# One-hot gate products written to neighbouring PSUM words, copied to SBUF by ScalarE and multiplied from there by VectorE

## The chip, the cores and the metric

The kernel runs on one core of a Trainium2 chip. The metric is the device time of one execution in microseconds (us). A core has the engines TensorE (PE, with its weight loads shown apart as PEld), VectorE (DVE), ScalarE (ACT), GpSimd (POOL) and SyncE (SP, which here only issues DMAs). Each engine works through a queue of instructions of its own.

## The reference, cut to what matters

The program is two transformer blocks on 256 tokens of width 1024. Only the end of the second block is touched by the change: a product-key expert layer with 16384 experts of which each token uses 8 x 16.

```python
s = einsum("thpd,hpnd->thpn", q, sub_keys)            # 8 heads, two halves of 128 keys
s_top, i_top = top_k(s, 16)
best, ci = top_k(s_top[..., 0, :, None] + s_top[..., 1, None, :], 16)
e = i1 * 128 + i2                                      # expert of token t, head h, rank k
gate = softmax(best)
act = gelu(einsum("thkd,td->thk", u_exp[e], xb))
out = einsum("thk,thkd->td", gate * act, v_exp[e])
```

## The kernel before, in words

The kernel gathers no expert. It computes gelu(u . x) for all 16384 experts and all 256 tokens, multiplies each by the gate that the token gives to that expert (zero for nearly all), and multiplies the result by all of v. The products of gelu are the *stash*: `ST[0]` and `ST[1]`, each 128 partitions x 64 experts x 256 tokens of float32, partition and column together being the expert's number.

The layer runs in three stages on TensorE:

- **u stage.** 64 chunks of 1 MB of `peer_u` come by DMA (`raw`). For each half chunk ScalarE rounds it to float32r (`whi`, line 128), VectorE computes the rest (`wlo`, line 129), and TensorE multiplies both parts with the tokens in 24 matmuls of 128x256 into the PSUM tile `mm`. ScalarE takes gelu of a chunk to the stash (line 1418 before, the same line after).
- **gates.** `weights8(half, t0)` makes the gates of 8 tokens for one half of the stash. There are 32 groups of 8 tokens and two halves, so 64 calls. VectorE builds one-hot matrices in the tile `one` (lines 1551, 1552) and multiplies one of them by the gate, which is split into three bfloat16 parts (line 1555, three times). TensorE multiplies them: for each token three accumulating bfloat16 matmuls with 128 weights columns (`B`) and 64 moving columns (`Aw`), 24 for a call and 1536 in all. Their result is the table of gates, 128 x 64 for each token, in one PSUM bank (tile `mb`, two of them). VectorE multiplies this bank with the stash in place (line 1562).
- **v stage.** The stash is split into two parts (`pTh` by ScalarE, `pTl` by VectorE, line 135), chunks of `peer_v` come and are split as those of u, and TensorE sums 12 matmuls of 128x512 for each half chunk into the tiles `acc`.

The gates of the first half are made while the second half of u is multiplied, those of the second half while the first half of v is. `one` has two buffers and `mb` two, so calls go in pairs: two calls are built, their 48 matmuls stand close together in TensorE's queue, and two multiplications follow. A pair's matmuls are mostly one run of 48 or 46 between the wide matmuls; the first one or two often stand alone.

The order within each engine's queue is set before the launch by a scheduler that works from a timeline of its own; `prio(...)` only shifts what it prefers. So an edit can move instructions that it does not name.

Of the kernel before, what the change touches and what calls it, by code (L numbers as in the profile page):

```python
# [10 lines left out]
F32 = mybir.dt.float32  # L11
# [4 lines left out]
AF = mybir.ActivationFunctionType  # L16
ALU = mybir.AluOpType
# [4 lines left out]
P = 128  # L22
# [39 lines left out]
def tile_kernel(ctx, tc, A, out, taps=None):  # L62
    nc = tc.nc
# [16 lines left out]
    def mmps(side=None):  # L80

        if side is None:
            turn[0] += 1
            side = turn[0] % turn[1] == 0
        if side:
            return psum.tile([P, 512], F32, name="mb", tag="mb", bufs=2)
        return psum.tile([P, 512], F32, name="mm", tag="mm", bufs=6)
# [4 lines left out]
    @contextmanager  # L92
    def prio(d):

        p = tc.cur_priority
        tc.cur_priority = max(0, p + d)
        try:
            yield
        finally:
            tc.cur_priority = p  # L100
# [44 lines left out]
    def mm(ps, lhsT, rhs, start, stop):  # L145
        nc.tensor.matmul(ps, lhsT, rhs, start=start, stop=stop, skip_group_check=True)  # L146
# [1250 lines left out]
    for c in range(3, 8):  # L1397
        hs = weights[c - 3] if c < 5 else q_halves(c)
        ps = mmps()
# [137 lines left out]
    def weights8(half, t0):  # L1537
        ps = mmps(True)
        n = 8
        one = pk.tile([P, n * 384], BF, name="one", tag="one", bufs=2)  # L1540
        B = one[:, :n * P].rearrange("p (t j) -> p t j", t=n)
        E = one[:, n * P:n * 192]
        Aw = one[:, n * 192:].rearrange("p (i t j) -> p i t j", i=3, t=n)

        def pairs(v, j):
            return v.rearrange("p (t j d) -> p t j d", t=n, d=2) if j is None else v.rearrange("p (j d) -> p j d", d=2)[:, None].to_broadcast([P, n, j, 2])

        def each(v, j):
            return v[:, t0:t0 + n, None, :].to_broadcast([P, n, j, 2])

        nc.vector.tensor_tensor(pairs(one[:, :n * P], None), pairs(iob, 64), each(iT[:, 1], 64), op=ALU.is_equal)
        nc.vector.tensor_tensor(pairs(E, None), pairs(iob[:, half * 64:(half + 1) * 64], 32), each(iT[:, 0], 32), op=ALU.is_equal)
        for i in range(3):
            o = n * 192 + i * n * 64
            nc.vector.tensor_tensor(pairs(one[:, o:o + n * 64], None), pairs(E, None), each(g3[:, i], 32), op=ALU.mult)
        po = ps.rearrange("p (i t) -> p i t", t=n)
        with prio(-2 * LOW):
            for t in range(n):
                for i in range(3):
                    mm(po[:, :, t], B[:, t, :], Aw[:, i, t, :], i == 0, i == 2)  # L1560
        v = ST[half][:, :, t0:t0 + n]
        nc.vector.tensor_tensor(v, po, v, op=ALU.mult)

    def v_split(c):
        half, o = c // 32, (2 * c) % 64
# [11 lines left out]
    with prio(LOW):  # L1577
        for t0 in range(0, T, 8):
            weights8(0, t0)
# [10 lines left out]
    with prio(LOW):  # L1590
        for t0 in range(0, T, 8):
            weights8(1, t0)
# [31 lines left out]
    for tt in range(NT):  # L1624
        ss = ev[:, 6 * D + 8 * tt:6 * D + 8 * tt + 2]
        for j in range(2):
            o = slice(j * 512, (j + 1) * 512)
            t = rt[tt][:, o]
# [102 lines left out]
```

## Time and profile before

| | |
|---|---|
| time, median of 3 runs | 1662.21 us (1661.76 to 1663.13) |
| profiled execution | 1662.13 us, span of the core 1660.4 us |
| granted TensorE clock | 0.999 of full speed |
| TensorE busy | 1637.8 us, 99% of the span |
| VectorE busy | 1183.4 us, 71% |
| ScalarE busy | 770.5 us, 46% |
| gate matmuls on TensorE | 1536, from 979 to 1434 us |

The span runs from the first to the last instruction; the 1.7 us between it and the profiled execution's time lie outside of it. TensorE's matmuls overlap and their ends are modelled, so the distance between the starts of matmuls tells more than their durations. A row of the timeline that ends in xN is N instructions of one kind with no idle time between them.

### The profile page before, as it was taken

The page shows a single profiled execution, that of the slowest core. Times are in us where ns is not written, and L with a number is a line of the kernel's source. Part 1 is how long each engine was busy: PE and PEld are TensorE (multiplying, and loading weights), DVE is VectorE, ACT ScalarE, POOL GpSimd, SP SyncE. Part 2 cuts the span into 40 slices and gives each one's busy share as a digit, 9 for nine tenths or more (in the row PEclk, how much of TensorE's full clock was granted, in tenths as well). Part 3 has the DMA queues.
Part 4 walks back from the last instruction along what each step waited for, and adds up shares of the span by engine and source line. Part 5 has one row for each costly group of instructions (what it writes and reads, how often), then busy time and mean ns, then how long its engine had stood idle before and what let it go on. Part 6 is the DMA issues. An engine that isn't in the chain of part 4 may idle for free.

```text
span 1660.4 us, 28789 instructions
## 1 busy us (share of the span) xinstructions
PE 1637.8 (99%) x12006; PEld 1515.3 (91%) x12006; DVE 1183.4 (71%) x1925; ACT 770.5 (46%) x1064; POOL 62.7 (4%) x114
## 2 busy tenths in 40 slices
PE   7999999999999999999999999999999999999997
PEld 7999999989999899998999999999999888888886
DVE  5768776666878676766799984877747888755555
ACT  5545444464544466653544444333344333454443
POOL 0000000200000010002000000000000000000001
PEclk9999999999999999999999999999999999999999
DMA  5739665235866455463535545344355434455553
GB/s 225 283 135 349 261 258 220 94 132 218 339 256 242 178 170 176 144 247 130 194 128 180 184 170 181 128 142 137 128 183 212 165 135 155 159 188 201 186 195 127
DMA packets 46274, 312.76 MB, mean 188 GB/s; under 512 B 6240, under 2 KB 6256, under 8 KB 10304
## 3 DMA queue, kind: packets, MB, share of 16 engines
q1 hardware_dynamic: 43344, 300.82, 50.7%
q0 software_dynamic: 2656, 9.06, 1.6%
q8 instruction: 94, 1.54, 0.4%
q10 hardware_dynamic: 144, 1.05, 0.2%
q14 instruction: 36, 0.29, 0.1%
HBM read 308.78 MB, written 2.12 MB: 187 GB/s over the span
## 4 chain that ended last, share of the span: by engine, by line
PE 95%; DVE 2%; DMA 1%; ACT 1%; POOL 0%; issue 0%; SPq 0%; POOLq 0%; DVEq 0%; ACTq 0%
PE mm L146 46%; PE acc L146 32%; PE mb L146 16%; PE mm L217 0%; DMA raw<-in_conv_w_in 0%; DMA raw<-in_mla_w_uq 0%; POOL xn L1219 0%; DVE wlo L129 0%; DVE first L135 0%; ACT pTh L135 0%; PE mb L217 0%; DVE stash L1629 0%; DVE stash L1630 0%; DVE xn L1230 0%; DVE hres L1217 0%
## 5 line engine op out<-in xcount | busy, mean ns | idle before, releaser
L129 DVE TENSOR_TENSOR wlo<-raw,whi 128x1024 fp32r<-128x1024 f32 x492 | 597.7, 1223 | 278.9 <-ACT whi L128 277.8
L128 ACT ACTIVATE whi<-raw 128x1024 fp32r<-128x1024 f32 x492 | 514.6, 1057 | 602.2 <-PE mm L146 360.5
L146 PE MATMUL mm<-pTh,whi 128*128 128x256 f32 x1720 | 489.0, 284 | 0.0
L146 PE MATMUL mm<-pTl,whi 128*128 128x256 f32 x1720 | 487.9, 284 | 0.0
L146 PE MATMUL mm<-pTh,wlo 128*128 128x256 f32 x1720 | 487.2, 284 | 0.0
L146 PEld LDWEIGHTS mm<-pTh,whi 128*128 128x128 f32 x1720 | 329.7, 192 | 1.5 <-issue 0.3
L146 PEld LDWEIGHTS mm<-pTl,whi 128*128 128x128 f32 x1720 | 329.9, 192 | 0.8
L146 PEld LDWEIGHTS mm<-pTh,wlo 128*128 128x128 f32 x1720 | 329.5, 192 | 0.5
L146 PE MATMUL acc<-wlo,pTh 128*128 128x512 f32 x512 | 159.4, 391 | 0.0
L146 PE MATMUL acc<-whi,pTl 128*128 128x512 f32 x512 | 158.3, 389 | 0.0
L146 PE MATMUL acc<-whi,pTh 128*128 128x512 f32 x512 | 145.1, 391 | 0.0
L146 PEld LDWEIGHTS acc<-whi,pTl 128*128 128x128 f32 x512 | 96.1, 188 | 20.1
L146 PEld LDWEIGHTS acc<-whi,pTh 128*128 128x128 f32 x512 | 96.2, 188 | 19.6
L146 PEld LDWEIGHTS acc<-wlo,pTh 128*128 128x128 f32 x512 | 95.6, 189 | 19.1
L146 PE MATMUL mb<-pTh,whi 128*128 128x256 f32 x392 | 111.2, 284 | 0.0
L146 PE MATMUL mb<-pTh,wlo 128*128 128x256 f32 x392 | 110.9, 283 | 0.0
L146 PE MATMUL mb<-pTl,whi 128*128 128x256 f32 x392 | 110.9, 283 | 0.0
L146 PE MATMUL mb<-one 128*128 128x64 bf16 x1536 | 98.1, 246 | 0.0
L146 PEld LDWEIGHTS <-one 128*128 128x128 bf16 x1536 | 87.4, 123 | 6.8 <-DVE wlo L129 2.9
L135 ACT ACTIVATE pTh<-stash 128x512 fp32r<-128x512 f32 x64 | 40.6, 634 | 90.6 <-PE acc L146 89.0
L146 PEld LDWEIGHTS mb<-pTh,whi 128*128 128x128 f32 x392 | 74.8, 191 | 0.6
L146 PEld LDWEIGHTS mb<-pTl,whi 128*128 128x128 f32 x392 | 74.8, 191 | 0.5
(533 smaller groups left out, 2141.5 us busy)
## 6 DMA issues: line engine op xcount, KB each, us to landing
raw<-in_peer_u SPq DMA_DIRECT2D x64, 1024.0 KB, 4.8
raw<-in_peer_v SPq DMA_DIRECT2D x64, 1024.0 KB, 4.8
raw<-in_conv_ffn_w SPq DMA_DIRECT2D x33, 1024.0 KB, 6.8
raw<-in_mla_ffn_w SPq DMA_DIRECT2D x33, 1024.0 KB, 6.8
raw<-in_w_ada SPq DMA_DIRECT2D x24, 1024.0 KB, 8.5
raw<-in_conv_w_in SPq DMA_DIRECT2D x11, 1024.0 KB, 6.4
raw<-in_w_peer_q SPq DMA_DIRECT2D x8, 1024.0 KB, 4.8
raw<-in_conv_w_out SPq DMA_DIRECT2D x4, 1024.0 KB, 11.8
```

The lines of the kernel that those rows point to most:

```text
L128: nc.scalar.activation(hi[:, :n], raw[:, a:a + n], AF.Copy)
L129: marks["chunk"] = nc.vector.tensor_sub(lo[:, :n], raw[:, a:a + n], hi[:, :n])
L135: return nc.scalar.activation(hi, src, AF.Copy), nc.vector.tensor_sub(lo, src, hi)
L146: nc.tensor.matmul(ps, lhsT, rhs, start=start, stop=stop, skip_group_check=True)
```

## The change

Before, the matmuls of token `t` wrote `po[:, :, t]`: 64 words, each 8 words after the last, since the token is the innermost index of the bank. After, they write `ps[:, t*64:(t+1)*64]`, 64 neighbouring words. The token becomes the outer index of the bank, and the stash has it innermost. So ScalarE copies the bank with the indices exchanged into `G`, 512 float32 words that lie in the first part of the tile `one` (the place of `B`, which is no longer needed then), and VectorE multiplies `G` instead of the bank with the stash.

```diff
@@ weights8(half, t0)
-        po = ps.rearrange("p (i t) -> p i t", t=n)
         with prio(-2 * LOW):
             for t in range(n):
                 for i in range(3):
-                    mm(po[:, :, t], B[:, t, :], Aw[:, i, t, :], i == 0, i == 2)
+                    mm(ps[:, t * 64:(t + 1) * 64], B[:, t, :], Aw[:, i, t, :], i == 0, i == 2)
+
+        G = one[:, :n * P].bitcast(F32)
+        nc.scalar.activation(G.rearrange("p (i t) -> p i t", t=n), ps.rearrange("p (t i) -> p i t", t=n), AF.Copy)
         v = ST[half][:, :, t0:t0 + n]
-        nc.vector.tensor_tensor(v, po, v, op=ALU.mult)
+        nc.vector.tensor_tensor(v, G.rearrange("p (i t) -> p i t", t=n), v, op=ALU.mult)
```

The multiplication is line 1562 before and 1564 after; the new copy is line 1562 after.

VectorE's queue in the u stage, one pair of calls before: the two multiplications with the banks `mb`, then the next pair's `one` (1551, 1552, 1555) with three `wlo` among them.

```order
L1562 TENSOR_TENSOR stash_9003<-mb,stash_9003 128x64x8 x2
L1551 TENSOR_TENSOR one<-iob,iT 128x1024
L1552 TENSOR_TENSOR one<-iob,iT 128x512
L1551 TENSOR_TENSOR one<-iob,iT 128x1024
L1552 TENSOR_TENSOR one<-iob,iT 128x512
L129 TENSOR_TENSOR wlo<-raw,whi 128x1024
L1555 TENSOR_TENSOR one<-one,g_8608 128x512 x6
L129 TENSOR_TENSOR wlo<-raw,whi 128x1024 x2
```

The same place after.

```order
L1564 TENSOR_TENSOR stash_9003<-one,stash_9003 128x64x8 x2
L1551 TENSOR_TENSOR one<-iob,iT 128x1024
L1552 TENSOR_TENSOR one<-iob,iT 128x512
L1551 TENSOR_TENSOR one<-iob,iT 128x1024
L1552 TENSOR_TENSOR one<-iob,iT 128x512
L129 TENSOR_TENSOR wlo<-raw,whi 128x1024
L1555 TENSOR_TENSOR one<-one,g_8608 128x512 x6
L129 TENSOR_TENSOR wlo<-raw,whi 128x1024 x2
```

Nothing moved here but the source of the multiplication, which now waits for ScalarE instead of TensorE. Before, pairs differ a little in where a `wlo` stands; after, all pairs of the u stage have this order.

ScalarE's queue in the u stage before: only roundings of u (`whi`, two for a chunk) and the gelu of each chunk (line 1418).

```order
L128 ACTIVATE whi<-raw 128x1024 x2
L1418 ACTIVATE stash_8606<-mm 128x512
L128 ACTIVATE whi<-raw 128x1024 x2
L1418 ACTIVATE stash_8606<-mm 128x512
L128 ACTIVATE whi<-raw 128x1024 x2
```

After, with the two copies of each pair.

```order
L128 ACTIVATE whi<-raw 128x1024
L1562 ACTIVATE one<-mb 128x512 x2
L128 ACTIVATE whi<-raw 128x1024
L1418 ACTIVATE stash_8606<-mm 128x512
L128 ACTIVATE whi<-raw 128x1024 x2
L1418 ACTIVATE stash_8606<-mm 128x512
L1562 ACTIVATE one<-mb 128x512 x2
L128 ACTIVATE whi<-raw 128x1024 x2
```

Two copies stand after every third rounding, and the next rounding stands behind them. In this stage TensorE's queue now has 72 wide matmuls for each pair of calls, 68 of them in one piece behind the long run; before there were 53 to 66.

TensorE's queue at a pair in the v stage before: the pair's 48 gate matmuls (`mb<-one`, each with its weight load) start behind four `acc` matmuls and stand in one run.

```order
L146 MATMUL acc<-whi,pTl 128x512 x2
L146 MATMUL acc<-whi,pTh 128x512 x4
L146 LDWEIGHTS one
L146 MATMUL mb<-one 128x64
L146 LDWEIGHTS one
L146 MATMUL mb<-one 128x64
L146 LDWEIGHTS one
L146 MATMUL mb<-one 128x64
```

A pair in the v stage after.

```order
L146 MATMUL acc<-whi,pTh 128x512 x4
L146 LDWEIGHTS one
L146 MATMUL mb<-one 128x64
L146 LDWEIGHTS one
L146 MATMUL mb<-one 128x64
L146 MATMUL acc<-wlo,pTh 128x512 x2
L146 MATMUL acc<-whi,pTl 128x512 x2
L146 MATMUL acc<-wlo,pTh 128x512 x2
L146 MATMUL acc<-whi,pTl 128x512 x2
L146 MATMUL acc<-whi,pTh 128x512 x3
L146 LDWEIGHTS one
L146 MATMUL mb<-one 128x64
```

Here two of the 48 stand ahead of eleven `acc` matmuls and 46 behind. Over both stages the 1536 gate matmuls stand in 71 runs before and in 81 after; between the pairs of the v stage stand 38 `acc` matmuls on average before and 42 after.

## Rows read from the trace of the kernel before

**Rows 1.** The page's first part: busy us, share of the span, instructions.

```profile
PE 1637.8 (99%) x12006; PEld 1515.3 (91%) x12006; DVE 1183.4 (71%) x1925; ACT 770.5 (46%) x1064; POOL 62.7 (4%) x114
```

**Rows 2.** By stretch: us, busy PE, PEld, DVE, ACT, POOL (instructions), clock, DMA, GB/s.

```profile
976.00:1258.00 282.00, 282.00 (x2763) 279.86 (x2763) 186.04 (x292) 105.99 (x123) 0.00 (x0) 1.00 0.45 153
1258.00:1440.00 182.00, 182.00 (x1352) 154.75 (x1351) 152.44 (x252) 70.92 (x83) 1.63 (x3) 1.00 0.46 159
```

**Rows 3.** Chain that ended last, in order of time: start us, us, what, count.

```profile
1050.30 5.92 PE mm L146 x49
1056.21 0.07 PE mb L146
1056.29 0.29 PE mm L146 x2
...
1056.93 2.58 PE mb L146 x46
1059.52 7.47 PE mm L146 x62
...
1281.16 2.70 PE mb L146 x48
1283.85 8.23 PE acc L146 x36
```

**Rows 4.** Timeline of PE, a run's first gate matmuls: start us, us, count.

```profile
1302.85 0.23 PE L146 MATMUL mb<-one 128*128 128x64 bf16 x1
...
1302.89 0.41 PE L146 MATMUL mb<-one 128*128 128x64 bf16 x4
...
1302.95 0.41 PE L146 MATMUL mb<-one 128*128 128x64 bf16 x4
```

**Rows 5.** Timeline of PE, single gate matmuls ahead of a run.

```profile
1056.06 0.23 PE L146 MATMUL mb<-one 128*128 128x64 bf16 x1
1056.10 0.36 PE L146 MATMUL mm<-pTh,whi 128*128 128x256 f32 x1
1056.30 0.28 PE L146 MATMUL mm<-pTl,whi 128*128 128x256 f32 x1
```

**Rows 6.** Weight loads of `one`: timeline of a run's start; ns min/median/max of all.

```profile
1302.85 0.12 PEld L146 LDWEIGHTS <-one 128*128 128x128 bf16 x2 [0.26 <-DVE wlo L129]
...
L146 PEld LDWEIGHTS <-one x1536: 95/125/125, 979.2 to 1433.6; 128*128 128x128 bf16 x192
```

**Rows 7.** Timeline of PEld where a run of gate matmuls ends.

```profile
985.30 0.22 PEld L146 LDWEIGHTS mm<-pTl,whi 128*128 128x128 f32 x1
985.44 0.19 PEld L146 LDWEIGHTS mm<-pTh,wlo 128*128 128x128 f32 x1
```

**Rows 8.** Timeline of DVE after a run of gate matmuls, with idle time before.

```profile
1059.50 1.29 DVE L1562 TENSOR_TENSOR stash<-mb,stash 128x512 f32<-128x512 f32 x2 [2.95 <-PE mb L146]
1060.70 0.68 DVE L1551 TENSOR_TENSOR one<-iob,iT 128x1024 bf16<-128x1024 bf16 x1
...
1062.58 1.22 DVE L129 TENSOR_TENSOR wlo<-raw,whi 128x1024 fp32r<-128x1024 f32 x1
1063.71 2.10 DVE L1555 TENSOR_TENSOR one<-one,g 128x512 bf16<-128x512 bf16 x6
```

**Rows 9.** Instructions of ScalarE and VectorE: ns min/median/max, first and last start.

```profile
L1418 ACT ACTIVATE stash<-mm x63: 577/581/600, 851.3 to 1256.4; 128x512 f32<-128x512 f32 x63
L128 ACT ACTIVATE whi<-raw x492: 632/1061/1112, 9.2 to 1643.2; 128x1024 fp32r<-128x1024 f32 x164
L1562 DVE TENSOR_TENSOR stash<-mb,stash x64: 680/686/694, 1033.3 to 1434.5; 128x512 f32<-128x512 f32 x64
```

**Rows 10.** Waits from 976 to 1440 us: us in total, times, longest.

```profile
ACT whi L128 <- PE mm L146: 169.6, 81, 4.9
...
DVE stash L1562 <- PE mb L146: 45.2, 30, 3.2
```

## Prediction

> **What bounds the kernel now.** The page comes first: TensorE is busy for 99% of the span, VectorE for 71%, ScalarE for 46% [rows 1]. An average over stages can hide a wait, so the two stretches in which gates are made come next: TensorE is busy in all 282 us of the one and all 182 us of the other, at a granted clock of 1.00, which is its level of 2.4 GHz [rows 2]. VectorE has 186.0 us of work in the first and 152.4 us in the second, 66% and 84%. So TensorE's work sets the time there, and an edit pays only by what it takes off TensorE or costs only by what makes TensorE wait.
>
> The chain in order of time prices TensorE's work. A run of 48 gate matmuls takes 2.70 us, one of 46 takes 2.58 us, 0.056 us for each [rows 3]. 62 wide matmuls of 256 columns take 7.47 us, 0.1205 each, and 36 of 512 columns take 8.23 us, 0.2286 each [rows 3]. The difference of the last two, 0.108 us for 256 columns, is 0.42 ns for a column, one column per cycle at 2.4 GHz, and leaves 13 ns that do not depend on columns. By columns alone a gate matmul of 64 would take 27 ns, and with those 13 ns 40 ns. It takes 56. Something doubles it.
>
> What that is must be read from a run's beginning. The second gate matmul starts 0.04 us after the first, but the third 0.06 us after the second, and so on [rows 4]. Where a gate matmul stands alone, the wide matmul behind it also starts 0.04 us later [rows 5]. So a gate matmul that has none of its kind ahead lets the next one in after 40 ns, of which some 10 are the wait for its own weights: the second weight load of a run ends 0.12 us after the first began, and a load takes 0.095 us at the least, so loads can follow each other within 0.02 us [rows 6]. That leaves 28 to 30 ns, which is the 27 of the columns. From the second on 27 ns more are missing in each, and the weight loads too take 125 ns at the median instead of 95 [rows 6]. The same delay meets a weight load of another kind: the wide matmul's load right behind a run takes 0.22 us, the next 0.19 us [rows 7]. I read this as the results of the matmul before, which still go to PSUM: 64 words, each 8 words from the last, at half the rate of the columns, 53 ns, plus the 2 to 3 that are left to 56.
>
> **The change part by part.** *Neighbouring words.* If this reading holds, the rate of the columns is left: 27 to 30 ns for each gate matmul within a run, and I take 29, the distance that the run's beginning shows without the wait for weights. The bounds are 27 ns below and 56 ns above (nothing is gained), with 40 between them if the 13 ns of the wide matmuls also belong to these. 1536 matmuls in 81 runs have 1455 distances; 1455 x (55.5 - 29) ns = 38.6 us. The second matmul of each of some 33 long runs starts after 40 ns already, which takes back 33 x 15 ns = 0.5 us. The Trainium skill, "PSUM — Partial Sum Buffer", section "Specifications (TRN2)", says that PSUM has cachelines of 8 bytes and that any access pattern that is not contiguous slows matmuls significantly; it gives no size.
>
> *More runs.* A gate matmul that stands alone takes 0.07 us, and the two wide ones behind it 0.29 us, where two of 0.1205 would take 0.24 [rows 3]: 0.12 us in all, 0.09 more than the 29 ns within a run. The order of the change has ten more runs: 10 x 0.09 = 0.9 us lost. If a run of two costs no more than a single one, it is half of that.
>
> *The copies.* No row shows ScalarE read a bank with the indices exchanged. The nearest is gelu of 512 words from PSUM to SBUF, 0.58 us [rows 9]; above it I set 1.06 us, the price of 1024 words [rows 9], as if each word cost two. I take 0.58, since count, source and destination are the same. 64 copies are 37 us, 68 at the upper bound, on an engine that works 106 of 282 us and 71 of 182 us in the two stretches [rows 2]: it has room. Queued behind a copy that waits for gate matmuls are the next roundings `whi`, and VectorE's `wlo` and then TensorE wait for those. They have slack: ScalarE itself waits 169.6 us for TensorE to release `whi` buffers in these stretches [rows 10].
>
> *The multiplication from SBUF.* It took 686 ns from PSUM [rows 9]. From SBUF a split of 1024 words takes 1.22 us [rows 8], 0.61 us for 512 by count, so 0.6 to 0.7 us: no change worth a term, and off the path, since VectorE waits 45.2 us for gate matmuls at just this line [rows 10].
>
> *Its new place behind the copy.* Before, the multiplication began at 1059.50 us, just when the chain has the run of gate matmuls end, 1059.52 [rows 3, 8]. The `wlo` ahead of the next gates was done 4.3 us after that, the first third of the next gates 4.6 us after it (1063.71 and a sixth of 2.10) [rows 8]. A copy ahead adds 0.58 us and, as I guess, 0.1 us for the second hand-over: 5.0 and 5.3 us. In the order of the change TensorE comes to the next gates after 68 wide matmuls, 68 x 0.1205 = 8.2 us, and first uses that `wlo` after some 57, 6.9 us. So a cover of 1.9 us at the narrowest hides the copy. Without it each of 31 pairs would lose the excess.
>
> *What comes next.* With some 37 us less of TensorE, VectorE's 152.4 us meet about 163 us instead of 182 in the v stage, 94%, and the order of the change puts 42 instead of 38 `acc` matmuls between pairs there, which spreads the gates over more time. It stays below TensorE, so I add nothing, and keep 0 to 6 us for waits of TensorE on single splits.
>
> The sum: 1660.4 - 38.6 + 0.5 + 0.9 = 1623.2 us of span; with the 1.7 us outside it the time is 1624.9 us. The profiled execution took 1662.13 us, the median is 1662.21, so no correction: **1625 us**.
>
> **The rivals.** *A: as above*, 1625 us; 27 ns instead of 29 take 2.9 us more and runs of two may cost 0.4 us less, some 1621 us, which I round down to 1620; 6 us of waits and 30 ns for each lead up to 1633 us.
>
> *B: only part is gained.* The 13 ns between wide matmuls are a price of changing weights that gate matmuls pay as well; then 40 ns remain: 1455 x 15.5 ns = 22.6 us, less 0.9: 1640 us. For it speaks that every wide matmul pays them; against it that loads of these smaller weights follow each other within 0.02 us [rows 6].
>
> *C: the change does not do what it says.* What doubles the gate matmul is its weight load, which must wait for the columns of the matmul before: 27 ns of columns, some 15 to 20 of load and 13 of the change of weights make 55 to 60 ns, also what is measured. Loads of 125 ns in a run speak for it [rows 6]; against it that the second load of a run is not held and that a wide load behind a run is [rows 6, 7]. Then nothing is gained, ten more runs cost some 0.8 us, and the time is 1663 us. The Trainium skill, "TensorE: Matmul & The Clock Gate", section "Back-to-back issue gap", speaks for this: it gives a stream of pairs of weight load and matmul about 81 ns at 128 columns, in place of 56 for the matmul alone. By that page an estimate for 64 columns, 64 cycles less, is 54 ns with no word on PSUM's strides, and the time would stay at 1663 us. No row here shows such pairs with neighbouring words, so the trace neither bears it out nor refutes it.
>
> *D: slower, by the way through ScalarE.* If the copy with exchanged indices is much slower than its count of words, the next pair's `wlo` comes late. Two copies of c us each, 0.1 us, the second multiplication with 0.6 us, the four instructions that begin `one` with 1.9 us (1060.70 to 1062.58) and a `wlo` with 1.2 us [rows 8] make 3.8 us + 2c against 6.9 us. TensorE begins to wait at c = 1.55 us, and at 2.15 us the wait of 1.2 us for each of 31 pairs eats A's 37 us. At four times 0.58, 2.3 us, it waits 1.5 us for each, 47 us, and the time is 1672 us. Against it: no row of ScalarE comes near such a price for 512 words.
>
> **How the numbers follow.** Chances: A 0.55, B 0.15, C 0.20, D 0.10. A measurement of this kernel can tell changes of about 0.2%, 3.3 us, from none. A and B are faster, 0.70; C is within 0.2%, 0.20; D is slower, 0.10. The likeliest case has 1620 to 1633 us by itself. It and B hold only 0.70, so the range must reach up to C: 1620 to 1664 us.
>
> **What would show it.** Right: gate matmuls in a run start 29 ns apart, a run of 46 takes some 1.35 us instead of 2.58, its weight loads have a median near 100 ns, the load behind a run takes 0.19 to 0.20 us; TensorE stays without idle time in both stretches, which are together some 37 us shorter; copies take 0.58 us. B shows 40 ns, C 56 ns and loads of 125 ns as before. D shows TensorE waiting for `wlo` or `one` behind each run, and copies of over 1.5 us. The prediction is wrong above all if the distance within a run does not change.

## The result, and the profile after

The change takes the kernel from 1662.18 us (1661.76 to 1663.13) to 1623.72 us, median of four runs (1623.70 to 1624.06): a ratio of 0.977, with a 95% interval of 0.9758 to 0.9782. The forecast was 1625 us. The profiled execution has a span of 1622.0 us, 38.4 us less than before, at a granted clock of 0.998.

First the page's busy times of after (as in [rows 1]).

```profile
PE 1599.9 (99%) x12006; PEld 1475.8 (91%) x12006; DVE 1180.8 (73%) x1925; ACT 804.1 (50%) x1128; POOL 62.6 (4%) x114
```

TensorE is still busy for 99%, with the same 12006 matmuls in 37.9 us less. ScalarE has the 64 copies more and works 33.6 us longer. Next the two stretches with gates, by the columns of [rows 2]. I let them meet at 1240 us, since the `mm` matmuls of the u stage end there now.

```profile
976.00:1240.00 264.00, 264.00 (x2781) 261.76 (x2781) 182.17 (x284) 125.30 (x159) 0.00 (x0) 1.00 0.48 164
1240.00:1440.00 200.00, 200.00 (x1498) 164.65 (x1497) 175.50 (x281) 104.29 (x131) 1.63 (x3) 1.00 0.52 180
```

TensorE has no idle time in either, again at the level of 2.4 GHz. So the time left through TensorE's own work, and nothing took its place. Both kernels are busy with the gates within the same 464 us, and in them the kernel after starts 774 `acc` matmuls, where the kernel before started 605. 169 more, at 0.227 us each, are 38 us, so the gain lies inside these stretches, as the prediction has it. Which work became shorter is told by the same view for the instructions of tile `one` alone, from 976 to 1440 us: before,

```profile
976.00:1440.00 464.00, 98.13 (x1536) 87.41 (x1536) 128.33 (x316) 1.00 0.46 155
```

and after, where ScalarE's 64 copies make one column more:

```profile
976.00:1440.00 464.00, 58.86 (x1536) 49.78 (x1536) 167.12 (x380) 34.79 (x64) 1.00 0.50 171
```

The 1536 gate matmuls (the first number behind the stretch's length) take 39.3 us less. That is with their ends as modelled; counted from each start to the next start on TensorE, 84.6 us became 45.6, 39.0 us less. The span is 38.4 us shorter, so 0.6 to 0.9 us went back to the matmuls around them. The chain of after, in order of time (start, us, what, count), shows the runs one by one.

```profile
1050.54 1.36 PE mb L146 x46
1051.90 8.22 PE mm L146 x68
1060.12 0.05 PE mb L146
1060.17 0.31 PE mm L146 x2
```

46 gate matmuls take 1.36 us instead of 2.58, the wide ones 0.121 us each as before [rows 3]. The starts at the head of one run come from the timeline of PE:

```profile
1070.98 0.38 PE L146 MATMUL mb<-one 128*128 128x64 bf16 x7
...
1071.02 0.37 PE L146 MATMUL mb<-one 128*128 128x64 bf16 x7
...
1071.05 0.37 PE L146 MATMUL mb<-one 128*128 128x64 bf16 x7
```

The second starts 0.04 us after the first, as before; the third 0.03 us after the second, where before it was 0.06 [rows 4]. Over the 1455 distances inside runs the starts lie 29 ns apart. Tile `one` by instruction (ns minimum/median/maximum) answers to [rows 6, 9]:

```profile
L146 PEld LDWEIGHTS <-one x1536: 95/98/101, 978.7 to 1414.8; 128*128 128x128 bf16 x192
...
L1562 ACT ACTIVATE one<-mb x64: 582/596/601, 983.9 to 1415.5; 128x512 f32<-128x512 f32 x64
L1564 DVE TENSOR_TENSOR stash<-one,stash x64: 681/687/694, 1031.7 to 1416.2; 128x512 f32<-128x512 f32 x64
```

Weight loads are down from 125 ns to 98 at the median. The loads are the same; I read the 27 ns as time in which they were held inside a run, and copy_only below bears that out. The copy takes 596 ns, the multiplication 687 instead of 686. The wide matmul's load right behind a run, 0.22 us before [rows 7], now costs what the next one does (timeline of PEld):

```profile
1072.31 0.19 PEld L146 LDWEIGHTS mm<-pTh,whi 128*128 128x128 f32 x1
...
1072.42 0.19 PEld L146 LDWEIGHTS mm<-pTl,whi 128*128 128x128 f32 x1
```

What follows that run on the two other engines answers to [rows 8]; the bracket is the idle time before, and what ended it. ScalarE:

```profile
1072.56 1.09 ACT L1562 ACTIVATE one<-mb 128x512 f32<-128x512 f32 x2 [1.99 <-issue]
```

and VectorE:

```profile
1073.19 1.30 DVE L1564 TENSOR_TENSOR stash<-one,stash 128x512 f32<-128x512 f32 x2 [1.72 <-ACT one L1562]
1074.40 0.69 DVE L1551 TENSOR_TENSOR one<-iob,iT 128x1024 bf16<-128x1024 bf16 x1
...
1076.28 1.22 DVE L129 TENSOR_TENSOR wlo<-raw,whi 128x1024 fp32r<-128x1024 f32 x1
1077.41 2.10 DVE L1555 TENSOR_TENSOR one<-one,g 128x512 bf16<-128x512 bf16 x6
```

The run ends at 1072.49 us (1070.98 and 1.51 for its 46 matmuls, as the timeline draws them). The multiplication starts 0.7 us later, `wlo` is done 5.0 us after the run's end, and the first third of the next gates 5.3 us after it (1077.41 and a sixth of 2.10). TensorE reaches them behind 68 wide matmuls, 8.22 us, and waits for nothing.

### The profile page after: what moved, and what is told of

It is laid out like the page before. It is cut to its first block, busy times and chain, and to the rows that moved or that the text cites. A ratio compares the mean times of both kernels' runs of the same rounds, so it can differ in the third digit from the quotient of the medians.

```text
span 1622.0 us, 28952 instructions
## 1 busy us (share of the span) xinstructions
PE 1599.9 (99%) x12006; PEld 1475.8 (91%) x12006; DVE 1180.8 (73%) x1925; ACT 804.1 (50%) x1128; POOL 62.6 (4%) x114
## 4 chain that ended last, share of the span: by engine, by line
PE 96%; DVE 2%; ACT 1%; issue 1%; DMA 0%; POOL 0%; SPq 0%; POOLq 0%; DVEq 0%
PE mm L146 48%; PE acc L146 33%; PE mb L146 14%; PE mm L217 1%; DMA raw<-in_conv_w_in 0%; DVE wlo L129 0%; DVE first L135 0%; ACT pTh L135 0%; PE mb L217 0%; DVE stash L1631 0%; DVE stash L1632 0%; DVE xn L1230 0%; DVE hres L1217 0%; ACT b4h L566 0%; DVE rt L1216 0%
## 5 line engine op out<-in xcount | busy, mean ns | idle before, releaser
L146 PEld LDWEIGHTS mb<-pTh,wlo 128*128 128x128 f32 x392 | 74.8, 191 | 0.0
L1555 DVE TENSOR_TENSOR one<-one,g 128x512 bf16<-128x512 bf16 x192 | 68.0, 416 | 0.0
```

## The experiments

The theory at this point: what doubled a gate matmul was the place of its 64 result words, 8 words apart, and nothing else in it (A). The rivals of the prediction are at hand: the weight load (C), a fixed price of changing weights (B), and the way through ScalarE (D). All kernels below compute the whole reference. Each is an edit of the kernel after the change; the kernel before had 1661.95 us beside the first four and 1661.90 beside the last four.

**The words without the copy (no_copy).** Matmuls write neighbouring words, and VectorE reads PSUM itself with the indices exchanged.

```diff
-        G = one[:, :n * P].bitcast(F32)
-        nc.scalar.activation(G.rearrange("p (i t) -> p i t", t=n), ps.rearrange("p (t i) -> p i t", t=n), AF.Copy)
         v = ST[half][:, :, t0:t0 + n]
-        nc.vector.tensor_tensor(v, G.rearrange("p (i t) -> p i t", t=n), v, op=ALU.mult)
+        nc.vector.tensor_tensor(v, ps.rearrange("p (t i) -> p i t", t=n), v, op=ALU.mult)
```

> Gate matmuls write 64 neighbouring words as in the change, but VectorE multiplies the bank itself with the stash, exchanging the indices while it reads, and there is no copy by ScalarE. TensorE's queue has the 71 runs of the kernel before. Theory (the step between the written words is all that matters): matmuls in a run stand 29 ns apart, and the time is that of the change less ten split runs, 1623.7 - 0.9 = 1622.8 us. Rival (the copy is needed, since VectorE reads exchanged words from PSUM slowly): the multiplication takes 1.2 us or more instead of 0.69, VectorE is late in the v stage, and the time is over 1630 us.

1623.14 us (1622.79 to 1623.40), ratio 0.9766 (0.975 to 0.9783). Gate matmuls start 29 ns apart. The multiplication, in its group by instruction:

```profile
L1562 DVE TENSOR_TENSOR stash<-mb,stash x64: 678/682/693, 1031.9 to 1396.0; 128x512 f32<-128x512 f32 x64
```

The whole gain is there without the copy, and VectorE pays nothing for the exchanged read: 682 ns against 686 [rows 9]. ScalarE's 64 copies are hidden, but they buy nothing either.

**The copy without the words (copy_only).** Matmuls write every eighth word as before; the bank goes through ScalarE in its own order.

```diff
+        po = ps.rearrange("p (i t) -> p i t", t=n)
...
-                    mm(ps[:, t * 64:(t + 1) * 64], B[:, t, :], Aw[:, i, t, :], i == 0, i == 2)
+                    mm(po[:, :, t], B[:, t, :], Aw[:, i, t, :], i == 0, i == 2)
...
-        nc.scalar.activation(G.rearrange("p (i t) -> p i t", t=n), ps.rearrange("p (t i) -> p i t", t=n), AF.Copy)
+        nc.scalar.activation(G, ps, AF.Copy)
```

> Gate matmuls write words 8 apart as before, and ScalarE copies the bank in its own order to SBUF, from where VectorE multiplies. The queues have the change's order, with 81 runs. Theory: 56 ns between matmuls of a run, nothing gained by the copy, ten more runs cost 0.7 us: 1662.9 us, and at most 2 us more by waits. Rival (part of the gain comes from a bank that is free earlier or from VectorE's lighter read): 1650 us or less.

1662.82 us (1662.46 to 1663.53), ratio 1.0006 (0.9996 to 1.0015): no difference to before. Its chain and its tile `one` by instruction:

```profile
1053.03 2.58 PE mb L146 x46
```

```profile
L146 PEld LDWEIGHTS <-one x1536: 95/125/125, 978.9 to 1453.7; 128*128 128x128 bf16 x192
...
L1562 ACT ACTIVATE one<-mb x64: 591/597/599, 985.2 to 1454.4; 128x512 f32<-128x512 f32 x64
```

The loads, the copies and the split into 81 runs are those of the change; only the step between result words is that of before, and with it the 56 ns and the loads of 125 ns come back. That refutes C: the loads are the same as in the change and are long only with this step, so a load is long because it is held by the matmuls ahead, not the other way round. The copy takes as long in the bank's own order (597 ns) as with words 64 apart (596), so the exchange costs ScalarE nothing.

**Every second word (step_2).** The words of two tokens are interleaved; each matmul writes with a step of 2 instead of 8.

```diff
-                    mm(ps[:, t * 64:(t + 1) * 64], B[:, t, :], Aw[:, i, t, :], i == 0, i == 2)
+                    mm(ps[:, (t // 2) * P + t % 2:(t // 2 + 1) * P:2], B[:, t, :], Aw[:, i, t, :], i == 0, i == 2)
...
-        nc.scalar.activation(G.rearrange("p (i t) -> p i t", t=n), ps.rearrange("p (t i) -> p i t", t=n), AF.Copy)
+        nc.scalar.activation(G.rearrange("p (i a b) -> p a i b", a=n // 2, b=2), ps.rearrange("p (a i b) -> p a i b", a=n // 2, b=2), AF.Copy)
```

> As the change, but two tokens share 128 words of the bank, one on the even words and one on the odd: the words of a matmul are 2 apart instead of 1. Theory of lines (what costs is that no two written words in a row share 8 bytes): 56 ns in a run, as with 8 apart, and 1662.9 us. Rival (the cost grows with the distance between words): between 29 and 56 ns, near 33 ns for 2 against 8, some 1630 us.

1662.91 us (1662.48 to 1663.30), ratio 1.0005 (0.9996 to 1.0015). Again 2.58 us for 46:

```profile
1053.32 2.58 PE mb L146 x46
```

A step of 2 costs what a step of 8 costs. The price does not grow with the distance; it is there as soon as words are not neighbours.

**Neighbours in twos, far apart (two_and_jump).** Each matmul writes 32 pairs of neighbouring words, each pair beginning at an even word, 16 words from one pair to the next.

```diff
-                    mm(ps[:, t * 64:(t + 1) * 64], B[:, t, :], Aw[:, i, t, :], i == 0, i == 2)
+                    mm(ps.rearrange("p (i t d) -> p t i d", t=n, d=2)[:, t], B[:, t, :], Aw[:, i, t, :].rearrange("p (i d) -> p i d", d=2), i == 0, i == 2)
...
-        nc.scalar.activation(G.rearrange("p (i t) -> p i t", t=n), ps.rearrange("p (t i) -> p i t", t=n), AF.Copy)
+        nc.scalar.activation(G.rearrange("p (i d t) -> p i d t", d=2, t=n), ps.rearrange("p (i t d) -> p i d t", t=n, d=2), AF.Copy)
```

> As the change, but a matmul writes two neighbouring words, jumps over 14, writes two, and so on, 32 times. Theory of lines: each 8 bytes are filled by two words in a row, so 29 ns in a run as with 64 neighbouring words, and 1623.7 us. Rival (any pattern that is not one piece is slow, or the distance counts): 56 ns and 1662.9 us, or between.

1624.15 us (1623.81 to 1624.47), ratio 0.9772 (0.9756 to 0.9788).

```profile
1051.24 1.36 PE mb L146 x46
```

The 29 ns are there, with jumps of 64 bytes between pairs. So the 64 words need not be in one piece; pieces of two words are enough.

**Pairs that begin at odd words (two_across).** The same pairs 16 words apart, but moved by one word; the eighth token takes words 0 and 15 of each block of 16.

```diff
+        blk = ps.rearrange("p (i w) -> p i w", w=16)
...
-                    mm(ps[:, t * 64:(t + 1) * 64], B[:, t, :], Aw[:, i, t, :], i == 0, i == 2)
+                    mm(blk[:, :, 2 * t + 1:2 * t + 3] if t < 7 else blk[:, :, 0:16:15], B[:, t, :], Aw[:, i, t, :].rearrange("p (i d) -> p i d", d=2), i == 0, i == 2)
...
-        nc.scalar.activation(G.rearrange("p (i t) -> p i t", t=n), ps.rearrange("p (t i) -> p i t", t=n), AF.Copy)
+        Gb = G.rearrange("p (i d t) -> p i d t", d=2, t=n)
+        nc.scalar.activation(Gb[:, :, :, :7], blk[:, :, 1:15].rearrange("p i (t d) -> p i d t", d=2), AF.Copy)
+        nc.scalar.activation(Gb[:, :, :, 7], blk[:, :, 0:16:15], AF.Copy)
```

> As two words and a jump of 14, but each two neighbouring words begin at an odd word (tokens 0 to 6), so that they lie in two different pieces of 8 bytes; token 7 takes the first and last word of each 16. Two ScalarE copies instead of one, 96 runs. Theory of lines (aligned pieces of 8 bytes): no two words in a row share a line, 56 ns in a run, 1662.9 + 15 x 0.07 = 1664 us. Rival (any two neighbours are enough): 29 ns for seven of eight tokens, some 1630 us.

1664.01 us (1663.76 to 1664.15), ratio 1.0012 (1.0002 to 1.0021), the 2 us above before with 96 runs instead of 71.

```profile
1053.14 2.58 PE mb L146 x46
```

Neighbouring words are not enough. Both words must lie in one aligned piece of 8 bytes; two pieces for two words cost the 56 ns.

**Fewer runs (parts_reversed).** VectorE makes the three gate parts in the other order. The part that TensorE needs last is then no longer made last, and in the order of this kernel 36 runs, nearly all of 48, take the place of 81.

```diff
-        for i in range(3):
+        for i in (2, 1, 0):
```

> As the change, but VectorE multiplies the three parts of the gates last part first, so that the first gate matmul of a pair, which needs the first part, can only stand in the order behind all three. TensorE's queue then has 36 runs, nearly all of 48, instead of 81: 45 single ones or runs of two are gone. Theory (each single one costs 0.09 us more than within a run): 1623.7 - 45 x 0.09 = 1619.7 us. Rival (a single one costs only its place, or TensorE now waits for the last part): 1623 to 1625 us.

1619.92 us (1619.60 to 1620.33), ratio 0.9747 (0.9734 to 0.9761). Its chain in both stretches:

```profile
1050.89 1.42 PE mb L146 x48
1052.30 8.94 PE mm L146 x74
...
1252.38 1.42 PE mb L146 x48
1253.80 11.00 PE acc L146 x48
```

45 runs less save 3.8 us against the change, 0.084 us for each. That is the price of leaving the stream and coming back, which the prediction took as 0.09.

**Both (reversed_no_copy).** The two edits, parts_reversed and no_copy, together.

```diff
-        for i in range(3):
+        for i in (2, 1, 0):
...
-        nc.vector.tensor_tensor(v, G.rearrange("p (i t) -> p i t", t=n), v, op=ALU.mult)
+        nc.vector.tensor_tensor(v, ps.rearrange("p (t i) -> p i t", t=n), v, op=ALU.mult)
```

> As the last one, and without ScalarE's copy: VectorE multiplies the bank itself. 36 runs instead of the 71 of the kernel without a copy. Theory: 1623.1 - 35 x 0.09 = 1620.0 us, no other than with the copy. Rival (with full runs of 48 the shorter way without the copy keeps TensorE from waiting): more than 1 us faster than with the copy.

1619.92 us (1619.76 to 1620.05), ratio 0.9747 (0.9733 to 0.9761), the same as with the copy. Of the versions that beat both kernels this is the simplest: no copy, 36 runs.

**The copy four times (four_copies).** It asks where the copies' cover ends, and whether D would have come true at four times 0.58 us.

```diff
-        nc.scalar.activation(G.rearrange("p (i t) -> p i t", t=n), ps.rearrange("p (t i) -> p i t", t=n), AF.Copy)
+        for _ in range(4):
+            nc.scalar.activation(G.rearrange("p (i t) -> p i t", t=n), ps.rearrange("p (t i) -> p i t", t=n), AF.Copy)
```

> As the change, but ScalarE makes each copy four times over, 192 copies more, about 115 us more work for it. The order changes with it: 117 runs instead of 81, mostly single calls instead of pairs. Theory (the way through ScalarE is covered as long as the order leaves room, and only the split runs cost): 1623.7 + 36 x 0.09 = 1627 us. Rival D (behind four copies the next pieces come late): TensorE waits over 1 us for each of some 60 groups, 1670 us or more.

1661.33 us (1660.94 to 1662.15), ratio 0.9998 (0.9988 to 1.0007): neither what the theory nor what D expected. Gate matmuls still start 29 ns apart at the full clock, so the whole gain was made and then lost again elsewhere. The stretches, by the columns of [rows 2], show where:

```profile
976.00:1240.00 264.00, 264.00 (x2751) 259.98 (x2751) 183.17 (x280) 180.29 (x257) 0.00 (x0) 1.00 0.48 161
1240.00:1440.00 200.00, 196.03 (x1331) 161.99 (x1329) 155.37 (x232) 130.76 (x190) 1.62 (x3) 1.00 0.54 189
1440.00:1480.00 40.00, 19.73 (x210) 15.87 (x211) 25.12 (x54) 21.84 (x38) 0.00 (x0) 0.53 0.00 1
```

In the first stretch, D's place, TensorE waits for nothing. It stands still around 1440 us. Its timeline there:

```profile
1434.46 1.57 PE L146 MATMUL mb<-one 128*128 128x64 bf16 x48
1443.17 3.28 PE L146 MATMUL mb<-one 128*128 128x64 bf16 x48 [7.14 <-DVE one L1555]
...
1451.40 4.07 PE L146 MATMUL mb<-one 128*128 128x64 bf16 x48 [4.95 <-DVE one L1555]
...
1458.29 2.00 PE L146 MATMUL mb<-one 128*128 128x64 bf16 x24 [2.82 <-ACT one L1563]
...
1474.00 1.22 PE L146 MATMUL acc<-whi,pTh 128*128 128x512 f32 x2 [3.96 <-ACT pTh L135]
```

The second half of the v stage needs all gates of its half of the stash. In the order of this kernel the last 240 gate matmuls (five pairs of calls) stand where no `acc` work of the first half is left to lie between them: all 768 `acc` matmuls of that half have started before 1434.5 us. Each pair's chain of gates, matmuls, copies and multiplication then stands bare: 39.5 us from 1434.5 to 1474.0 for matmuls that need 7.0 us at 29 ns, 32.5 us lost. The 117 runs instead of 81 account for 36 x 0.084 = 3.0 us more. Together that is 35.5 of the 37.3 us by which its span (1659.3 us) exceeds that of the change. In those 32.5 us TensorE is not idle throughout; part of them is the clock. Two runs in the chain, the first ahead of the idle times and the second behind 7.14 us of it:

```profile
1434.62 1.44 PE mb L146 x48
...
1443.84 2.62 PE mb L146 x46
```

and the stretch of the second, by the columns of [rows 2]:

```profile
1443.10:1446.50 3.40, 3.06 (x48) 2.68 (x48) 1.69 (x6) 1.21 (x3) 0.00 (x0) 0.50 0.02 5
```

At the granted clock of 0.50, its level of 1.2 GHz, the gate matmuls come 57 ns apart (2.62 / 46) instead of 29; for the 192 behind the first run that makes up to 192 x 28 ns = 5.4 us. The clock also covers the rest of the 37.3 us: the first nine `acc` matmuls behind the last wait take 4.0 us, from 1474.00 us to the tenth's start at 1478.01, where 9 x 0.227 would be 2.0 us.

The change itself keeps clear of this. The last links of its chain are

```profile
1072.50 8.22 PE mm L146 x68
...
1414.99 193.90 PE acc L146 x855
```

The `acc` matmuls behind its last run of gates are 855 in this chain and 18 more, which start after the chain has left TensorE: 873 of the stage's 1536. 768 of them (half of the 1536) are the second half's, so 105 x 0.227 = 24 us of the first half's work lie behind the last gates.

## Why the prediction was right

*What bounds the kernel.* TensorE, without idle time, before and after. An edit that took 39.3 us off its work took 38.4 off the span.

*The cause.* I read the doubling from the head of a run, where the second matmul is not held: the results of the matmul ahead, not its weights. The runs bear that out against both rivals. C falls with copy_only and step_2, in which, for TensorE, only the step of the words differs from kernels at 29 ns. B falls with the distance itself, 29 ns where it gave 40. The Trainium skill, "TensorE: Matmul & The Clock Gate", section "Back-to-back issue gap", spoke for C with an estimate of 54 ns for 64 columns from its 81 ns at 128; 29 ns were measured for such pairs, and the measurement decides. How the results hold up TensorE is not settled: whether the matmul itself goes at half the rate or the next one waits for its words to be written would read the same in these rows.

*The size.* The 29 ns taken from a run's head were met: 1.36 us for 46 against "some 1.35", loads of 98 ns at the median against "near 100", 0.19 us for the load behind a run. The two terms for the gate matmuls, 38.6 and 0.5, make 38.1 us, where the distances between starts gave 39.0. Two slips stand in that sum, and the smaller one hides part of the larger. It counts only distances inside runs, but the last matmul of a run holds up the wide one behind it as well: for the 32 long runs that distance fell from 56 to 29 ns, which is 0.9 us more. And the second matmul of a long run starts 39 ns after the first in both kernels, so this distance gives back nothing: by the prediction's own reading 32 x 26.5 ns = 0.8 us had to be taken back, not 0.5. Why 29 and not the 27 of the columns alone stays open.

*More runs.* The 0.9 us of the sum is met as far as it can be told: 38.4 us of span against 39.3 or, by starts, 39.0 us of gate matmuls leaves 0.6 to 0.9, and parts_reversed gives 0.084 us a run by itself. The ten runs are not a price of the copy's time as such but of the order that it leads to: no_copy, with 71, is 0.6 us faster.

*The copy.* 596 ns against the 0.58 taken, hidden as argued: `wlo` 5.0 us and the gates 5.3 us after the run's end, as predicted. The upper bound of 1.06 us, two words' price for each, is refuted for this read.

*D.* Its price was not met, since the copy costs what its words cost. Its wait did not come at four copies either, 2.3 us in all, for which it gave each of 31 pairs of the u stage 1.5 us: there was none in that stage. But the order changed with the copies. Single calls took the place of most pairs there, mostly with 27 to 48 wide matmuls from one to the next, where D's sum has pairs and 68. So that sum, in the order that it was made for, stays untested. In the order of four_copies enough other work lay between, and the cost came at the border between the halves of the v stage. The prediction looked only at the distance from one pair to the next and named no such deadline; for the change it made no difference, since 24 us of cover were left. The sum, 1623.2 us of span, missed the measured 1622.0 by 1.2 us, 0.9 of them in the gate matmuls.

## What to carry to other kernels

Look at how a matmul's results lie in PSUM, not only at its operands: where words went out singly here, a matmul of 64 columns in a TensorE-bound stage took 56 ns instead of 29, and the exchange can be left to the engine that reads the bank (here VectorE, at no cost). To find out what holds a stream of equal instructions, look at its head, where nothing of its kind is ahead yet. And when an edit makes a chain longer under an order of due times, look for the last place at which its results are needed, since its slack there is not that of the steady state.

## What was not expected of the hardware

The rule for PSUM is sharper than "neighbouring words". At 64 words for each matmul, steps of 2 and 8 words and pairs that begin at odd words all give 56 ns, and pairs in aligned 8 bytes with 64 bytes from one to the next give the full 29 ns. The Trainium skill, "PSUM — Partial Sum Buffer", section "Specifications (TRN2)", has the lines of 8 bytes, and the runs agree; its remark that any pattern that is not contiguous slows matmuls is too wide, as two_and_jump shows.

ScalarE's read is free of it: 596 ns with words 64 apart, 597 in order. Of the copies of a whole bank only that of step_2 took longer, 682 ns. It reads the bank in order and is the only one of these that writes its SBUF words out of order, in pairs 8 words apart. So the write is the likelier cause, but no run tests it alone.

```profile
L1562 ACT ACTIVATE one<-mb x64: 661/682/719, 985.5 to 1454.8; 128x512 f32<-128x512 f32 x64
```

And a stall of TensorE cost more here than its own length: behind the first wait of four_copies the clock stood at 0.50, and 46 gate matmuls took 2.62 us instead of 1.36.
